# Another order for the end of the second mixer: two pairs of heads in a row, and the convolution's end among the output projection's blocks

## The chip, the cores and the metric

One core of one Trainium2 chip runs the whole program. The metric is the time of one execution in device microseconds: the median of several runs, and beside them one execution that the hardware profiler recorded.

## The reference

The input is 256 rows of 1024 values in float32. The reference sends them through two blocks. The first block has two layers of feed-forward, a mixer of three kinds of attention, and feed-forward. The second block, in which the change lies, has two layers of another mixer (`hybrid_layer`), each of which adds its result to the rows:

```python
o_a = fox_attention(...) * jax.nn.silu(f_gate)             # 4 heads of 64: blocks 0, 1 of the mix
o_b = conformer_conv(glu_in, ...) * jax.nn.silu(c_gate)    # 256 channels: blocks 2, 3
o_c = nsa_attention(...) * jax.nn.silu(n_gate)             # 8 heads of 64: blocks 4 to 7
return x + jnp.concatenate([o_a, o_b, o_c], axis=-1) @ w_out
```

`conformer_conv` gates its input, runs a causal convolution of 31 taps over the 256 rows in each of 256 channels, normalizes each row over its channels, applies SiLU and multiplies by a 256x256 matrix (`conv_pw`). Each head of `nsa_attention` has three terms: compressed keys, the selected keys (at this length all keys) and a window (again all keys). The last two are two causal softmaxes over 256 keys with different keys and values. The mix of 1024 columns is then multiplied by `w_out`, 1024x1024.

## The kernel before

The rows lie in two tiles of 128 partitions. A float32 product is taken as three matmuls of rounded parts: each factor is split into a high part (`L270` or, for weights, `L107`, on ACT) and a low part (`L271`, `L108`, on DVE), and `mm3` (`L237` to `L241`) multiplies low by high, high by high and high by low. Weights come through one stream of blocks (`Stream`): an SP DMA into `raw`, then `L107` and `L108`, with buffers that come round after seven blocks, so that a weight's cast waits for the matmuls of the block seven places earlier. The queues of the engines are filled by a scheduler that takes the order of the program text and a priority for each instruction; what the engine then does is the order that it was given.

A layer of the second mixer runs its input projections first, with some of the 62 taps (31 for each of two halves of the channels, `L1314`, on DVE) put between them: 40 of them are issued by the time that the part begins which the change touches. From there these pieces are in the text:

- `nsa_pair(p)`, two heads: `first` has the scores of the two softmaxes on PE (`L576`, into PSUM tiles `xt` of which there are three), the bias and the running minimum on DVE (`L584`), the exponentials on ACT (`L592`), the reciprocals and the weights on DVE (`L1214`, `L1217`, `L597`). `second` has one matmul for the compressed term (`L1225`, into the one tile `ot`), for each of the four weighted matrices three transposes on PE (`L267`, into an `xt`) and a copy on ACT (`L608`), the products with the values (`L615`, `L617`), and `gated_out` (`L1194`, `L270`, `L271`), which writes block 4 + p of the mix, `mT`, in two parts.
- `attend` issues the `first` of a pair and then the `second` of the pair before it; `settle` issues a `second` that is still waiting.
- `conv(n)` issues the next n taps. `conv_norm` transposes the 256 channels by 256 rows on PE, takes mean and variance of each row (`L1328`, `L1329`, and `L276`, `L277` on POOL) and normalizes into `yn` (`L1331`), one row tile after the other. `conv_silu` transposes back, scales (`L1341`), takes a tanh on ACT (`L1342`), multiplies (`L1344`) and splits into `R` (`L270`, `L271`). `conv_out` has twelve matmuls of 256 columns by `conv_pw` (`L245` to `L247`), then for two blocks `L1356`, `L270` and `L271`, which write blocks 2 and 3 of the mix.
- `outs(j)` multiplies one block of the mix by its 128 rows of `w_out`, in the order `OUT_ORDER = (0, 1, 4, 5, 2, 3, 6, 7)`: twelve matmuls of 512 columns, into four PSUM tiles `acc` that are held for all eight blocks. `finish_phase` has the last four blocks: 24 matmuls for the first row tile, then its residual and norm, then 24 for the second.

Before the change the end of the layer is written as pair 0, all the remaining 22 taps, pair 1, two output blocks, `conv_norm`, pair 2, an output block, `conv_silu`, pair 3, `conv_out`, an output block, the last `second`.

Of the kernel before, what the change touches and what calls it, by code (L numbers as in the profile page):

```python
# [138 lines left out]
class Kernel:  # L139
# [805 lines left out]
    def mixer2_stream(self, l):  # L945
        I, st = self.ins, self.st
        w = I["w_in_2"][l]
        self.xs_spec(w, 2308, 512)
        self.xs_spec(w, 2820, 280)
        self.xs_spec(w, 1796, 512)  # L950

        def with_hidden(c0, n):

            w1 = I[f"cmp_{n}_w1_2"][l].rearrange("(j p) f -> p j f", p=128)
            for i in range(2):
                self.ws_spec(w, c0 + 256 * i, 256)
                for j in (2 * i, 2 * i + 1):
                    st.add(w1[:, 4 * j:4 * j + 4, :], 4, 256)

        with_hidden(1028, "k")  # L960
        self.xs_spec(w, 512, 260)
        with_hidden(0, "v")
        self.ws_spec(w, 3100, 256)
        self.ws_spec(w, 772, 256)
        self.ws_spec(w, 3356, 256)
        self.ws_spec(w, 1540, 256)
        wo = I["w_out_2"][l].rearrange("(k p) f -> p k f", p=128)
        for i, k in enumerate(self.OUT_ORDER):
            if i == 3:
                st.add(I["conv_pw_2"][l].rearrange("(k p) f -> p k f", p=128), 2, 256)  # L970
            st.add(wo[:, k:k + 1, :], 1, 1024)

# [2 lines left out]
    def mixer2(self, l, src, pre, nxt, mid, late):  # L975
# [216 lines left out]
        def gated_out(k, o, gate):  # L1192
            y = self.gt(512)[:, :256]
            nc.vector.scalar_tensor_tensor(y, o, 0.5, gate, op0=OP.mult, op1=OP.mult)  # L1194
            self.split(mT[0][:, k], mT[1][:, k], y)
# [3 lines left out]
        def nsa_pair(p):  # L1199
            g = p // 2  # L1200
            pp = []

            def first():
                pp.extend([self.p384() for _ in range(2)] for _ in range(2))
                s = self.small(24)
                low, den, w = (s[:, i:i + 8].rearrange("p (m i b) -> p m i b", m=2, i=2) for i in (0, 8, 16))
                for i in range(2):
                    sc = self.scores([qT[r, p] for r in HALVES], [kT[r, g, i] for r in HALVES])
                    for m in range(2):
                        self.biased(pp[i][m], sc[m], self.table(4), 1.0, low[:, m, i])  # L1210
                for i in range(2):
                    for m in range(2):
                        self.exps(pp[i][m], low[:, m, i], den[:, m, i])
                nc.vector.reciprocal(s[:, 16:24], s[:, 8:16])  # L1214
                for m in range(2):
                    h = 2 * p + m
                    nc.vector.tensor_tensor(w[:, m], w[:, m],  # L1217
                                            gs[:, :, 3 * h + 1:3 * h + 3].rearrange("p b i -> p i b"), op=OP.mult)
                for i in range(2):
                    for m in range(2):  # L1220
                        self.weighted(pp[i][m], w[:, m, i])

            def second():
                o = self.pair_out()
                nc.tensor.matmul(o(), lhsT=vbd[:, 2 * p:2 * p + 2].rearrange("p a b -> p (a b)"), rhs=pcT,  # L1225
                                 start=True, stop=False)
                pts = [self.turn(pp[i], "aa") for i in range(2)]
                for i in range(2):
                    c = (384, 640)[i] + 64 * g
                    self.values(o, pts[i], [[nk[:, t, c:c + 64] for t in range(2)]] * 2, False, i == 1)  # L1230
                gated_out(4 + p, o(), sn[:, p])

            self.attend((first, second))
# [60 lines left out]
        def silu_gate(dst):  # L1294
            def f(i, a):
                d = dst[:, 2 * i:2 * i + 2]
                t = self.gt(2, 256)
                nc.scalar.activation(t, a, AF.Tanh, scale=0.5)
                nc.vector.scalar_tensor_tensor(d.rearrange("p a b -> p (a b)"), t.rearrange("p a b -> p (a b)"), 1.0,
                                               a.rearrange("p a b -> p (a b)"), op0=OP.add, op1=OP.mult)  # L1300
            return f
# [5 lines left out]
        def conv(n):  # L1307
            for _ in range(min(n, len(taps))):
                f, j = taps.pop(0)
                y = ypad[:, f, j:j + 256]  # L1310
                if j == 0:
                    nc.vector.tensor_scalar(yc[:, f], y, col(f, 0), col(f, 31), op0=OP.mult, op1=OP.add)
                else:
                    nc.vector.scalar_tensor_tensor(yc[:, f], y, col(f, j), yc[:, f], op0=OP.mult, op1=OP.add)  # L1314
# [5 lines left out]
        def conv_norm():  # L1320
            tp = self.cut(self.xt(), (2, 256))
            for t in range(2):
                for f in range(2):
                    self.transpose(tp[:, t, 128 * f:128 * f + 128], yc[:, f, 128 * t:128 * t + 128])
            yn.append(self.sb("yn", [2, 256], 1))
            s = self.small(24)
            for t in range(2):
                nc.vector.bn_stats(s[:, 6 * t:6 * t + 6], tp[:, t])  # L1328
                nc.vector.bn_aggr(s[:, 12 + 2 * t:14 + 2 * t], s[:, 6 * t:6 * t + 6])  # L1329
                self.rstd(s[:, 16 + t:17 + t], s[:, 13 + 2 * t:14 + 2 * t])  # L1330
                nc.vector.tensor_scalar(yn[0][:, t], tp[:, t], s[:, 12 + 2 * t:13 + 2 * t], s[:, 16 + t:17 + t],  # L1331
                                        op0=OP.subtract, op1=OP.mult)
# [28 lines left out]
        def out(i, t):  # L1361
            q = slice(128 * t, 128 * t + 128)
            k = self.OUT_ORDER[i]
            if not d:
                d.extend([self.acc(512), self.acc(512)] for _ in range(2))
            while len(W) <= i:
                W.append(st.next())
            for n in range(2):
                c = slice(512 * n, 512 * n + 512)
                self.mm3(d[t][n], (mT[0][:, k, q], mT[1][:, k, q]), tuple(x[:, 0, c] for x in W[i]), i == 0, i == 7)  # L1370

        def outs(*js):
            for i in js:
                for t in range(2):
                    out(i, t)
# [30 lines left out]
        conv(8)  # L1406
        self.ws_proj3(src, silu_gate(sc_), 0)
        nsa_pair(0)
        conv(62)
        nsa_pair(1)  # L1410
        outs(0, 1)
        conv_norm()
        nsa_pair(2)
        outs(2)
        conv_silu()
        nsa_pair(3)
        conv_out()
        outs(3)
        self.settle()
        self.close_inner()  # L1420
        late()
        self.finish_phase(lambda i, t: out(4 + i, t), 4, d, 1.0, nxt)
# [98 lines left out]
```

## Time and profile before

| | us |
|---|---|
| runs, median of 3 | 1621.61 |
| lowest, highest | 1618.85, 1622.76 |
| profiled execution | 1624.3 |
| span of the profiled execution, first to last instruction | 1622.5 |

The profiled execution lies 2.7 us above the median of the runs, and 1.8 us of it lie around its span. In the span the first block ends at about 1273 us and the first layer of the second block at about 1447 us; its second layer ends with the program. A timeline row gives the start in us from the span's start, the duration, engine, line, operation, output and input with their shapes, how many instructions were merged, and in brackets the idle time of the engine before it and what ended it. The matmuls of PE overlap by pipelining, so a step on PE is best taken from start to start.

### The profile page before, as it was taken

The numbers are of one execution on the slowest core, as the hardware profiler recorded it, in microseconds if no ns is written. First come the engines' busy times: TensorE is split into PE (matmuls) and PEld (weight loads), VectorE is DVE, ScalarE is ACT, GpSimd is POOL, SyncE is SP. The second block draws the span as 40 slices with busy tenths as digits, with TensorE's granted clock in tenths as the row PEclk, the third lists the DMA queues.
The fourth block names the chain that finished last, engine by engine and source line by source line (L and its number), as shares of the span: only waits on it lengthen the run. The fifth ranks groups of instructions, "written<-read, shape, count | busy, mean of one in ns | idle before, by whom it ended". The sixth has DMA issues, their size and how long they took to land.

```text
span 1622.5 us, 23859 instructions
## 1 busy us (share of the span) xinstructions
PE 1576.8 (97%) x8874; PEld 1325.5 (82%) x8874; DVE 1112.3 (69%) x2144; ACT 894.2 (55%) x1619; POOL 45.1 (3%) x66
## 2 busy tenths in 40 slices
PE   7999999999999999999999999999999999899988
PEld 5888888787878888788889787888888799579966
DVE  5756566667776665665656667787566579877985
ACT  5655455566665554555545655765555465555454
POOL 0000000001000000000010001000000000000000
PEclk9999999999999999999999999999999999899989
DMA  8776546454667664766636444468665375137601
GB/s 268 237 230 185 140 134 182 121 143 120 190 212 234 188 192 122 244 191 186 184 98 187 137 134 140 138 207 268 187 194 165 100 209 189 53 83 216 206 29 39
DMA packets 204300, 271.12 MB, mean 167 GB/s; under 512 B 10382, under 2 KB 172056, under 8 KB 204184
## 3 DMA queue, kind: packets, MB, share of 16 engines
q1 hardware_dynamic: 203752, 268.56, 55.9%
q8 instruction: 69, 1.13, 0.3%
q10 hardware_dynamic: 432, 1.05, 0.2%
q14 instruction: 47, 0.39, 0.1%
HBM read 268.52 MB, written 1.05 MB: 166 GB/s over the span
## 4 chain that ended last, share of the span: by engine, by line
PE 82%; DVE 7%; DMA 4%; ACT 4%; issue 2%; POOL 1%; SPq 0%; DVEq 0%; POOLq 0%; ACTq 0%
PE acc L252 28%; PE acc L253 14%; PE xt L241 4%; PE xt L240 4%; PE xt L239 4%; PE xt L267 4%; PE acc L239 3%; PE acc L240 3%; PE acc L241 3%; PE ot L615 2%; PE xt L576 2%; DVE w L108 2%; ACT w L107 2%; PE acc L245 1%; PE acc L247 1%
## 5 line engine op out<-in xcount | busy, mean ns | idle before, releaser
L108 DVE TENSOR_TENSOR w<-raw,w 128x1024 fp32r<-128x1024 f32 (+4 forms) x520 | 610.0, 1180 | 287.2 <-ACT w L107 277.5
L107 ACT CAST w<-raw 128x1024 fp32r<-128x1024 f32 (+4 forms) x520 | 525.5, 1014 | 317.5 <-PE acc L253 92.4
L252 PE MATMUL acc<-h,w 128*128 128x512 f32 x1824 | 649.2, 397 | 0.0
L253 PE MATMUL acc<-h,w 128*128 128x256 f32 x1824 | 515.8, 283 | 0.0
L252 PEld LDWEIGHTS acc<-h,w 128*128 128x128 f32 x1824 | 343.7, 188 | 78.8 <-issue 1.3
L253 PEld LDWEIGHTS acc<-h,w 128*128 128x128 f32 x1824 | 343.0, 188 | 3.8 <-issue 2.5
L239 PE MATMUL acc<-w,h 128*128 128x512 f32 (+5 forms) x448 | 168.4, 377 | 1.5 <-DVE h L271 1.0
L240 PE MATMUL acc<-w,h 128*128 128x512 f32 (+5 forms) x448 | 165.9, 370 | 0.0
L241 PE MATMUL acc<-w,h 128*128 128x512 f32 (+5 forms) x448 | 165.2, 369 | 0.5 <-DVE w L108 0.5
L257 ACT COPY gt<-acc 128x256 f32<-128x256 f32 x240 | 88.3, 373 | 139.1 <-PE acc L253 138.8
L258 DVE TENSOR_TENSOR gt<-gt,acc 128x256 f32<-128x256 f32 x240 | 98.7, 417 | 57.4 <-ACT gt L257 56.4
L239 PE MATMUL xt<-w,R 128*128 128x512 f32 x264 | 103.3, 391 | 1.2 <-DVE R L271 1.2
L240 PE MATMUL xt<-w,R 128*128 128x512 f32 x264 | 103.2, 391 | 0.0
L241 PE MATMUL xt<-w,R 128*128 128x512 f32 x264 | 103.1, 391 | 0.0
L239 PEld LDWEIGHTS acc<-w,h 128*128 128x128 f32 x448 | 85.5, 191 | 20.7 <-DVE h L271 3.8
L241 PEld LDWEIGHTS acc<-w,h 128*128 128x128 f32 x448 | 85.4, 191 | 14.0 <-DVE w L108 1.2
L240 PEld LDWEIGHTS acc<-w,h 128*128 128x128 f32 x448 | 85.3, 191 | 12.4 <-issue 0.5
L592 ACT ACTIVATE p<-p,small 128x128 f32<-128x128 f32 (+1 forms) x176 | 77.9, 445 | 20.5 <-DVE small L584 12.8
L245 PE MATMUL acc<-h,w 128*128 128x256 f32 x256 | 71.8, 281 | 0.0
L246 PE MATMUL acc<-h,w 128*128 128x256 f32 x256 | 71.7, 280 | 0.0
L247 PE MATMUL acc<-h,w 128*128 128x256 f32 x256 | 71.5, 279 | 0.0
L576 PE MATMUL xt<-G 64*128 64x128 f32 (+3 forms) x352 | 55.7, 356 | 5.0 <-DVE small L584 4.4
(256 smaller groups left out, 1926.7 us busy)
## 6 DMA issues: line engine op xcount, KB each, us to landing
raw<-in_w_in_dram SPq DMA_DIRECT2D x144, 512.0 KB, 4.3
raw<-in_ffn_w_gate_dram SPq DMA_DIRECT2D x88, 512.0 KB, 4.5
raw<-in_ffn_w_up_dram SPq DMA_DIRECT2D x88, 512.0 KB, 4.5
raw<-in_ffn_w_down_dram SPq DMA_DIRECT2D x88, 512.0 KB, 4.3
raw<-in_w_out_dram SPq DMA_DIRECT2D x32, 512.0 KB, 3.9
raw<-in_cmp_k_w_dram SPq DMA_DIRECT2D x8, 512.0 KB, 3.7
raw<-in_cmp_v_w_dram SPq DMA_DIRECT2D x8, 512.0 KB, 4.7
raw<-in_w_in_dram SPq DMA_DIRECT2D x8, 416.0 KB, 3.3
```

The costliest lines, as they stand in the source:

```text
L107: nc.scalar.copy(wh, raw)
L108: nc.vector.tensor_sub(wl, raw, wh.bitcast(F32))
L239: nc.tensor.matmul(out, lhsT=al, rhs=bh, start=first, stop=False)
L240: nc.tensor.matmul(out, lhsT=ah, rhs=bh, start=False, stop=False)
L241: nc.tensor.matmul(out, lhsT=ah, rhs=bl, start=False, stop=last)
L245: nc.tensor.matmul(out, lhsT=ah, rhs=bl, start=first, stop=False)
L247: nc.tensor.matmul(out, lhsT=al, rhs=bh, start=False, stop=last)
L252: nc.tensor.matmul(out, lhsT=ah, rhs=rhs, start=first, stop=False)
L253: nc.tensor.matmul(out[:, 1], lhsT=al, rhs=rhs[:, 0], start=False, stop=last)
L257: self.nc.scalar.copy(dst, a[:, 1])
L258: self.nc.vector.tensor_add(dst, dst, a[:, 0])
L576: nc.tensor.matmul(st[m][:, c], lhsT=qs[m][:, at:at + 128], rhs=ks[m][:, 0:n], start=True, stop=True)
```

## The change

The 22 taps that were left are cut in two: ten behind pair 1, the rest behind pair 2. Pair 1 follows pair 0 directly. `conv_norm` comes behind pair 3, an output block is moved ahead of `conv_silu`, and the last `second` ahead of `conv_out`. In the weight stream `conv_pw` trades places with the fourth block of `w_out`, as the new order takes them. The same instructions are issued.

```diff
--- before.py
+++ after.py
@@ -966,7 +966,7 @@
         self.ws_spec(w, 1540, 256)
         wo = I["w_out_2"][l].rearrange("(k p) f -> p k f", p=128)
         for i, k in enumerate(self.OUT_ORDER):
-            if i == 3:
+            if i == 4:
                 st.add(I["conv_pw_2"][l].rearrange("(k p) f -> p k f", p=128), 2, 256)
             st.add(wo[:, k:k + 1, :], 1, 1024)
 
@@ -1406,17 +1406,18 @@
         conv(8)
         self.ws_proj3(src, silu_gate(sc_), 0)
         nsa_pair(0)
+        nsa_pair(1)
+        conv(10)
+        outs(0, 1)
+        nsa_pair(2)
         conv(62)
-        nsa_pair(1)
-        outs(0, 1)
+        outs(2)
+        nsa_pair(3)
         conv_norm()
-        nsa_pair(2)
-        outs(2)
+        outs(3)
         conv_silu()
-        nsa_pair(3)
+        self.settle()
         conv_out()
-        outs(3)
-        self.settle()
         self.close_inner()
         late()
         self.finish_phase(lambda i, t: out(4 + i, t), 4, d, 1.0, nxt)
```

What this makes of the queues is the same in both layers but for single rows; the second layer is shown. First DVE, behind the weights of pair 0 (`L597`). `L1194` and `L271` belong to the heads before that pair; `L584` is the bias of pair 1, and each of its instructions has a second row for the minimum that it reads out; `G` with `conv` as input is a tap. Before:

```order
L597 TENSOR_SCALAR p<-p,small 128x256
L1194 SCALAR_TENSOR_TENSOR gt<-ot,G 128x256
L1314 SCALAR_TENSOR_TENSOR G<-G,conv 128x256 x2
L271 TENSOR_TENSOR h_69<-gt,h_69 128x256
L1314 SCALAR_TENSOR_TENSOR G<-G,conv 128x256 x14
L584 ISA p,small<-xt,base 128x128
L584 ISA small 128x1
L584 ISA p,small<-xt,base 128x256
```

Now:

```order
L597 TENSOR_SCALAR p<-p,small 128x256
L1194 SCALAR_TENSOR_TENSOR gt<-ot,G 128x256
L584 ISA p,small<-xt,base 128x128
L584 ISA small 128x1
L584 ISA p,small<-xt,base 128x256
L584 ISA small 128x1
L271 TENSOR_TENSOR h_69<-gt,h_69 128x256
L584 ISA p,small<-xt,base 128x128
L584 ISA small 128x1
L584 ISA p,small<-xt,base 128x256
```

The sixteen taps that stood ahead of pair 1's bias are gone from there. One of its four biases has moved ahead of the weights of pair 0, and the others follow `L1194`.

Next PE near the layer's end; `p` in `L267` are transposes of a pair's weighted matrices, `G` and `yn` those of the convolution, `w_14174` is the first of the last four blocks of `w_out`. Before, from the last transposes of pair 2 to the first product of `conv_out`:

```order
L267 MATMUL xt<-ident,p 128x128 x3
L615 MATMUL ot<-pt,G 64x256 x2
L617 MATMUL ot<-pt,G 64x128 x2
L615 MATMUL ot<-pt,G 64x256 x2
L617 MATMUL ot<-pt,G 64x128 x2
L245 MATMUL xt<-R,w_14059 128x256
L246 MATMUL xt<-R,w_14059 128x256
L247 MATMUL xt<-R,w_14059 128x256
```

Now, from the end of pair 2's products with the values to the same place:

```order
L617 MATMUL ot<-pt,G 64x128 x2
L267 MATMUL xt<-ident,G 128x128 x4
L1225 MATMUL ot<-G 128x256
L267 MATMUL xt<-ident,yn 128x128
L267 MATMUL xt<-ident,p 128x128 x6
L267 MATMUL xt<-ident,yn 128x128 x3
L267 MATMUL xt<-ident,p 128x128 x6
L615 MATMUL ot<-pt,G 64x256 x2
L617 MATMUL ot<-pt,G 64x128 x2
L615 MATMUL ot<-pt,G 64x256 x2
L617 MATMUL ot<-pt,G 64x128 x2
L245 MATMUL xt<-R,w_14064 128x256
```

The transposes of the convolution (`G` and `yn`) stood among the pairs, far ahead of this place. Now both stand behind the products of pair 2, and the transposes and products of pair 3, which followed `conv_out`, stand among and ahead of it. `conv_out` is followed at once by the last four blocks.

Last ACT, around the tanh of the convolution (`L1342`). Before:

```order
L608 COPY pt<-xt 128x384 x4
L270 CAST h_69<-gt 128x256
L1342 ACTIVATE gt<-gt 128x512
L592 ACTIVATE p,small<-p,small 128x128
L592 ACTIVATE p,small<-p,small 128x256
L592 ACTIVATE p,small<-p,small 128x128
L270 CAST R<-gt 128x512
L592 ACTIVATE p,small<-p,small 128x256
```

Now:

```order
L592 ACTIVATE p,small<-p,small 128x256
L608 COPY pt<-xt 128x384 x4
L270 CAST h_69<-gt 128x256
L608 COPY pt<-xt 128x384 x4
L1342 ACTIVATE gt<-gt 128x512
L270 CAST R<-gt 128x512
L270 CAST h_69<-gt 128x256 x3
```

The tanh stood ahead of pair 3's exponentials. Now it stands behind them and behind eight copies, four of pair 2 and four of pair 3. In the first layer casts of the next weights stand here too: an `L107` ahead of each of two `L270`, and, as before, an `L107` and an `L108` between `L1356` and the `L271` that ends the convolution.

## Rows read from the trace of the kernel before

**Rows 1.** The page, part 1: busy us, share of the span, instructions, by engine.

```profile
PE 1576.8 (97%) x8874; PEld 1325.5 (82%) x8874; DVE 1112.3 (69%) x2144; ACT 894.2 (55%) x1619; POOL 45.1 (3%) x66
```

**Rows 2.** Waits of PE, 1558 to 1623 us: waiter, releaser, us in total, times, longest.

```profile
PE xt L576 <- DVE small L584: 3.0, 1, 3.0
```

**Rows 3.** Windows: length, busy us (records) by engine, granted clock, DMA share, GB/s.

```profile
1394.00:1397.00 3.00, 3.00 (x7) 1.99 (x8) 3.00 (x9) 0.11 (x1) 0.00 (x0) 0.50 0.01 3
...
1573.00:1576.00 3.00, 2.78 (x12) 1.79 (x10) 2.68 (x10) 3.00 (x14) 0.00 (x0) 0.50 0.02 5
...
1576.00:1579.00 3.00, 3.00 (x15) 1.93 (x17) 2.86 (x12) 1.17 (x3) 0.00 (x0) 0.50 0.01 3
...
1606.00:1609.00 3.00, 3.00 (x14) 2.44 (x13) 0.00 (x0) 0.00 (x0) 0.00 (x0) 1.00 0.36 124
```

**Rows 4.** Timeline of DVE, second layer: start, us, engine, line, operation, tiles, count.

```profile
1556.54 0.28 DVE L584 CUSTOM_DVE_ANT_0 p<-xt,base 128x128 f32<-128x128 f32 x1
...
1558.76 1.67 DVE L1314 SCALAR_TENSOR_TENSOR G<-G,conv 128x256 f32<-128x256 f32 x4
...
1562.79 1.92 DVE L597 TENSOR_SCALAR p<-p,small 128x128 f32<-128x128 f32 x8
...
1564.63 0.42 DVE L1194 SCALAR_TENSOR_TENSOR gt<-ot,G 128x256 f32<-128x256 f32 x1
...
1566.08 5.63 DVE L1314 SCALAR_TENSOR_TENSOR G<-G,conv 128x256 f32<-128x256 f32 x14
```

**Rows 5.** Timeline of ACT, second layer.

```profile
1558.14 0.40 ACT L592 ACTIVATE p<-p,small 128x128 f32<-128x128 f32 x1
...
1561.65 0.83 ACT L608 COPY pt<-xt 128x384 f32<-128x384 f32 x2
...
1575.48 1.21 ACT L608 COPY pt<-xt 128x384 f32<-128x384 f32 x3
...
1592.17 0.63 ACT L1342 ACTIVATE gt<-gt 128x512 f32<-128x512 f32 x1 [1.15 <-DVE gt L1341]
...
1596.74 1.59 ACT L608 COPY pt<-xt 128x384 f32<-128x384 f32 x4
```

**Rows 6.** Timeline of DVE, second layer, the convolution's end.

```profile
1580.27 0.43 DVE L1328 BATCH_NORM_STATS2 small<-xt 128x6 f32<-128x256 f32 x1
...
1583.84 0.18 DVE L1329 BATCH_NORM_AGGREGATE small<-small 128x2 f32<-128x6 f32 x1
...
1585.02 0.54 DVE L1331 TENSOR_SCALAR yn<-xt,small 128x256 f32<-128x256 f32 x1 [0.68 <-POOL small L277]
...
1590.74 0.54 DVE L1341 TENSOR_SCALAR gt<-xt,conv 128x256 f32<-128x256 f32 x1 [0.16 <-PE xt L267]
...
1594.61 0.69 DVE L271 TENSOR_TENSOR R<-gt,R 128x512 fp32r<-128x512 f32 x1 [0.18 <-ACT R L270]
...
1600.86 0.76 DVE L1356 SCALAR_TENSOR_TENSOR gt<-xt,G 128x256 f32<-128x256 f32 x2 [0.25 <-PE xt L247]
```

**Rows 7.** Timeline of PE, second layer.

```profile
1564.01 1.66 PE L576 MATMUL xt<-G 64*128 64x128 f32 x8
...
1590.05 0.66 PE L267 MATMUL xt<-ident,yn 128*128 128x128 f32 x4
...
1599.18 0.39 PE L245 MATMUL xt<-R,w 128*128 128x256 f32 x1
...
1604.49 0.50 PE L240 MATMUL acc<-w,h 128*128 128x512 f32 x1
```

**Rows 8.** Timeline of PE, first layer, the first of the last 48 matmuls.

```profile
1434.77 0.50 PE L239 MATMUL acc<-w,h 128*128 128x512 f32 x1
```

**Rows 9.** Timeline of ACT, first layer.

```profile
1426.62 1.58 ACT L608 COPY pt<-xt 128x384 f32<-128x384 f32 x4
...
1430.74 1.05 ACT L107 CAST w<-raw 128x1024 fp32r<-128x1024 f32 x1 [0.71 <-PE xt L247]
```

**Rows 10.** Timeline of DVE, first layer.

```profile
1431.82 1.22 DVE L108 TENSOR_TENSOR w<-raw,w 128x1024 fp32r<-128x1024 f32 x1
```

## The prediction

> **What bounds the kernel now.** I read the page first: PE is busy for 97% of the span [rows 1], so time can only come from PE's waits and from its clock. The waits of PE at the second layer's end come next: its longest is 3.0 us, on the bias `L584` [rows 2]. The DVE timeline shows why: pair 1's scores run on PE from 1564.01 and take 1.66 us [rows 7], but DVE has fourteen taps from 1566.08 to 1571.7 ahead of the bias [rows 4]. The table by windows gives the second half of the cost: after the wait the granted clock is 0.50, the lower of the two levels (1.2 of 2.4 GHz), from 1573 to 1579, with PE busy nearly all the while [rows 3]. Last I read each engine's queue around the places that change, because all engines work their queues in order here.
>
> My reference in each layer is the moment when 48 matmuls of the output projection are left, all of `finish_phase`: from there on both kernels do the same. In the first layer that is 1434.77 [rows 8]. In the second 47 are left at 1604.49 [rows 7]; one matmul is 0.23 us at the full clock (13 weight loads in 3 us [rows 3]), so the moment is 1604.26.
>
> **What the change removes: taps ahead of pairs.** I add up DVE's new queue with durations of the second layer. A tap is 0.40 (5.63 by 14), the bias of a pair 2.22 (1556.54 to 1558.76), the weights of a pair 1.84 (1562.79 to 1564.63), `L1194` with `L271` 0.65 (1564.63 to 1566.08 less two taps) [rows 4], a weight's `L108` 1.2 [rows 10]. Reciprocal and `L1217` are 0.34: from the copies' start at 1561.65 [rows 5], which follows the last exponential, to 1562.79, less two taps. The exponentials of a pair take 3.5 on ACT (1558.14 to 1561.65) [rows 5]. The first of pair 1's four biases now falls into DVE's wait for pair 0's exponentials, so nothing moves until pair 0's weights end at 1564.63. Then:
>
> - `L1194`, `L271` and three biases; the last of these needs the third and fourth score tile, half as much again on PE as before (1564.01 + 2.5 = 1566.5), so DVE has done them by about 1567.6 and four taps by 1569.2.
> - Pair 1's last exponentials stand on ACT behind pair 0's first copy and end at about 1569.6. Reciprocal, tap, `L108`, weights: 1573.4.
> - `L1194`, `L271`, pair 2's bias: 1576.3. Its exponentials begin at about 1574.4 and end at 1577.9; 0.34, three taps, weights: about 1581.0.
> - `L1194`, `L271`, nine taps: 1585.3. Then pair 3's bias; its exponentials start 0.6 later and end at **1589.4**.
>
> Before they end at 1596.74, where the copies begin [rows 5]. So pair 3's softmax comes 7.3 us earlier. In the first layer two casts of 1.05 us [rows 9] stand ahead of `L270` on ACT and the clock is at its lower level for longer (0.50 at 1394 to 1397 [rows 3]); I take 1.5 us for that and get 1419.5 against 1426.62 [rows 9].
>
> **What it adds: a serial end.** Before, from pair 3's exponentials to the reference it is 7.5 us (1596.74 to 1604.26) and 8.15 us (1426.62 to 1434.77): copies, values, `conv_out`, and pair 3's transposes and values, behind which `conv_out`'s last steps are hidden. The norm of the convolution had been finished long before. Now the convolution's transposes stand on PE behind pair 2's values, and pair 2's copies on ACT behind pair 3's exponentials. From 1589.4 on each step waits for the one before it:
>
> 1. Copies, pair 2's values, transposes, until `L1328`: 4.8 us where the same steps ran mostly at the lower clock (1575.48 [rows 5] to 1580.27 [rows 6]); at the full clock 2.44 (1596.74 to 1599.18 [rows 5, 7]) and 0.7 for the transposes, 3.2.
> 2. The norm of two row tiles, DVE and POOL: 5.3 before (1580.27 to 1585.56), of which pair 2's biases between made up about 0.9; 4.4. From `L1329` to `L1331` it is 1.18 each time [rows 6].
> 3. Three transposes of `p`, whose PSUM tile is the one the norm has just read, then the last three of `yn`, until `L1341`: four transposes with the handover are 0.69 (1590.05 [rows 7] to 1590.74 [rows 6]) at the full clock; so 1.1, or 1.7 at half.
> 4. `L1341` twice: 1.0 [rows 6]. PSUM tiles are short again: pair 3's last six transposes need the tile that `L1341` reads, and the tanh stands on ACT behind their copies: 0.15 + 0.69 + two copies of 0.40 (1.21 by 3 [rows 5]), 1.5 to 2.1.
> 5. Tanh to the end of the split: 1592.17 [rows 5] to 1595.30 [rows 6], 3.1 with exponentials between; 2.9 to 3.1.
> 6. `conv_out` to the first matmul of the next block: 1.68 to `L1356` (1599.18 to 1600.86 [rows 7, 6]) and 1.4 for `L1356`, `L270`, `L271` and the handovers, 3.1; at half clock 4.4.
>
> The trace of before has no 256-column matmul at the lower clock; I bound step 6 by the full rate and by twice it. The Trainium skill ("TensorE: Matmul & The Clock Gate", section "Wait — 56ns, not 53.3ns?") gives columns over 1.2 GHz from start to start at that level, 0.213 us for 256 columns; by it the twelve take an estimated 2.6 us where the row has 1.4, and the step 4.3.
>
> The sum is 17.2 at the full clock and 21.5 at the lower one. PE mostly waits in this stretch, and after a wait of 3.0 us the row shows the lower clock; but it starts from the full one. I take **19.3**, near the middle. The first layer has a cast and an `L108` more in steps 1 and 6 (1.05 and 1.2 [rows 9, 10], half of it beside other work): 2.3 more, 21.6.
>
> Second layer: 1589.4 + 19.3 = 1608.7, against 1604.26: 4.4 later. First layer: 1419.5 + 21.6 = 1441.1, against 1434.77: 6.3 later.
>
> **The last 48 matmuls.** Before they run at 1.00 throughout. Now they start behind a wait on `L271`, at a clock that has seen little work. A half-clock stretch lasted at least 6 us [rows 3], and in it 7 matmuls run where else 13 do, so it takes half of its time. I take 4.5 us of it, 2.2 lost in each layer; bounds are 0 and 3.0.
>
> Moving the weights costs nothing: `conv_pw` and one block of `w_out` trade places on SP's queue, and the waits in these stretches are for PE, ACT and DVE, not for a transfer; if it were late, ACT's cast would hold up the copies behind it by as much. POOL's queue keeps its order.
>
> Sum: 4.4 + 6.3 + 2 x 2.2 = 15.1. On the profiled 1624.3 us that is 1639.4; that execution is 2.7 above the median, so **1636.7 us**.
>
> **Rivals.**
> - *The clock stays up.* If PE's waits are too short to lower it, the end costs 17.2 and 19.5: 1606.6 and 1439.0, 2.3 and 4.2 later, and the last 48 lose nothing: 1630.8 profiled, 1628 in the median. For it: the wait that lowers the clock before is one of 3.0 us, and the new ones are of 1 to 3. Against: there are five in a row.
> - *Gain and loss cancel.* The end breaks even at 14.9 us in the second layer and 15.3 in the first, some 2 to 4 below my full-clock sums. It needs pair 3's softmax to be done 2 us earlier than my DVE sum, which holds only 1 to 2 us of idle time, or the norm to be shorter. Then about 1622.
> - *The gain is kept: faster.* If the convolution's norm, tanh and split were done beside pair 3's softmax, the end would be 7.5 and 8.15 us as before, and all 7.3 and 7.1 us stay: 1607. It is decided by when `L1328` starts: at the last tap, 1585.3, or behind pair 2's values, 1592 to 1594. For it: the taps do end before pair 3's exponentials. Against it: the row of transposes on PE.
>
> **Chances.** Forecast 0.57, clock stays up 0.21, cancel 0.15, kept 0.07. What a measurement of this kernel can tell from no change is about 0.3%, 4.9 us. The first two cases lie above it but for a small part of the second: slower 0.76, same 0.16, faster 0.08. The forecast's own range, from a clock that is up most of the time to the lower one throughout (ends of 21.5 and 23.8: 6.6 and 8.5 later, and twice 3.0: 21.1 more), is 1629 to 1643. For 8 in 10 I go down into the cancelling case, to 1624, and up to 1644.
>
> **What would show it.** Right: the 3.0 us wait on `L584` is gone, pair 3's exponentials end 6 to 8 us earlier, near 1589 and 1419; behind them PE waits for copies, for `L1331` at the `yn` transposes, for the split before `L245`, and for `L271` at the first of the last blocks, with a granted clock of 0.50 in parts of it. Step by step: 19 us from pair 3's exponentials to the last 48 matmuls where it was 7.5. Wrong: exponentials that end after 1592 (the sum on DVE is too low) or before 1587; an end of under 15 us (the serial chain is not serial); the last 48 at 1.00 (no clock lost). In the median, a time under 1622 would refute the chain.

## The result and the profile after

The changed kernel takes 1633.03 us, median of 4 runs (1630.72 to 1634.08), against 1622.18 of the kernel before beside it: a ratio of 1.0072, 95% interval 1.0060 to 1.0085, or 10.9 us slower. In a second set it was 1631.57 (6 runs), ratio 1.0059 (1.0044 to 1.0074). The forecast was 1636.7 with a range of 1624 to 1644. The profiled execution took 1633.98 us, 1632.2 of it span. The work on PE is the same to a tenth [rows 1]:

```profile
PE 1576.8 (97%) x8874; PEld 1327.1 (81%) x8874; DVE 1111.8 (68%) x2144; ACT 894.0 (55%) x1619; POOL 51.0 (3%) x66
```

PE's busy time holds what the lower clock costs in either kernel, so the 9.7 us by which the span is longer are time in which PE waits. These are PE's waits after the change, waiter, releaser, us in total, times, longest; first the longest three of the first layer (1385 to 1455 us), then all of the second (1563 to 1633):

```profile
PE xt L267 <- DVE yn L1331: 3.2, 2, 3.0
PE acc L239 <- DVE h L271: 2.7, 1, 2.7
PE ot L615 <- ACT pt L608: 2.3, 1, 2.3
...
PE ot L615 <- ACT pt L608: 2.3, 1, 2.3
PE xt L267 <- DVE yn L1331: 1.9, 1, 1.9
PE xt L245 <- DVE R L271: 1.9, 1, 1.9
PE acc L239 <- DVE h L271: 1.4, 1, 1.4
PE xt L267 <- ACT pt L608: 1.1, 2, 0.6
```

The 3.0 us on `L584` [rows 2] are gone. In their place stand waits on the steps of the convolution: on `L1331` ahead of the `yn` transposes, on `R` ahead of `conv_out` and on the last `L271` ahead of the last 48 matmuls. (The 2.3 us on `L608` stand there before the change too.)

One new wait lies outside the part that the edit touches. In the first layer PE waits for a small copy on POOL (`L1149`, of the compressed keys), which took 1.94 us before the change:

```profile
1331.37 7.73 POOL L1149 COPY G<-G 32x64 f32<-32x64 f32 x1 [54.17 <-DVE G L1017]
```

```profile
PE xt L267 <- POOL G L1149: 2.7, 1, 2.7
```

A second profile of the changed kernel has 7.74 us and a wait of 2.4. From the copy's start to pair 0's copies on ACT it is 58.2 us in both, where it was 57.0. Whether the edit is what lengthens this copy is open; the last section comes back to it.

ACT after the change, the copies behind pair 3's exponentials in the first layer, and the same and the tanh in the second [rows 5, 9]:

```profile
1421.41 1.63 ACT L608 COPY pt<-xt 128x384 f32<-128x384 f32 x4
...
1597.57 1.63 ACT L608 COPY pt<-xt 128x384 f32<-128x384 f32 x4
...
1608.00 0.63 ACT L1342 ACTIVATE gt<-gt 128x512 f32<-128x512 f32 x1
```

DVE in the second layer, the steps of the serial end [rows 6]:

```profile
1600.73 0.43 DVE L1328 BATCH_NORM_STATS2 small<-xt 128x6 f32<-128x256 f32 x1 [0.16 <-PE xt L267]
...
1604.75 0.54 DVE L1331 TENSOR_SCALAR yn<-xt,small 128x256 f32<-128x256 f32 x1 [1.00 <-POOL small L277]
...
1606.29 1.00 DVE L1341 TENSOR_SCALAR gt<-xt,conv 128x256 f32<-128x256 f32 x2 [0.99 <-PE xt L267]
...
1610.04 0.69 DVE L271 TENSOR_TENSOR R<-gt,R 128x512 fp32r<-128x512 f32 x1 [0.35 <-ACT R L270]
```

PE: in the first layer the first of the last 48 matmuls and where they speed up, in the second the first and last product of `conv_out` and the first of the last 48 [rows 7, 8]:

```profile
1440.11 0.74 PE L239 MATMUL acc<-w,h 128*128 128x512 f32 x1 [2.73 <-DVE h L271]
...
1443.21 0.58 PE L240 MATMUL acc<-w,h 128*128 128x512 f32 x1
1443.63 0.39 PE L241 MATMUL acc<-w,h 128*128 128x512 f32 x1
...
1610.88 0.36 PE L245 MATMUL xt<-R,w 128*128 128x256 f32 x1 [1.86 <-DVE R L271]
...
1612.25 0.28 PE L247 MATMUL xt<-R,w 128*128 128x256 f32 x1
1613.94 0.50 PE L239 MATMUL acc<-w,h 128*128 128x512 f32 x1 [1.41 <-DVE h L271]
```

Windows of PE there: length, busy us (records), granted clock, DMA share, GB/s [rows 3].

```profile
1439.00:1442.00 3.00, 1.89 (x5) 0.70 0.55 131
1442.00:1445.00 3.00, 3.00 (x11) 0.73 0.02 8
1603.00:1606.00 3.00, 2.12 (x10) 0.67 0.00 0
1606.00:1609.00 3.00, 3.00 (x24) 0.76 0.00 0
1614.00:1617.00 3.00, 3.00 (x13) 1.00 0.00 0
```

Read so: from pair 3's last exponential to the last 48 matmuls it is 18.7 us in the first layer (1421.41 to 1440.11) and 16.4 in the second (1597.57 to 1613.94), where it was 8.15 and 7.5. In the first layer the last 48 start at the lower clock level, 0.42 us from one to the next until 1443.63; the residual behind the first 24 of them starts 6.74 us after the first, where it was 5.20, so 1.54 us are lost. In the second layer they run at 1.00 and lose nothing.

### The profile page after: what moved, and what is told of

Its sections match the earlier page's. It is cut to its first block, busy times and chain, and to the rows that moved or that the text cites. A ratio compares the mean times of both kernels' runs of the same rounds, so it can differ in the third digit from the quotient of the medians.

```text
span 1632.2 us, 23863 instructions
## 1 busy us (share of the span) xinstructions
PE 1576.8 (97%) x8874; PEld 1327.1 (81%) x8874; DVE 1111.8 (68%) x2144; ACT 894.0 (55%) x1619; POOL 51.0 (3%) x66
## 5 line engine op out<-in xcount | busy, mean ns | idle before, releaser
L108 DVE TENSOR_TENSOR w<-raw,w 128x1024 fp32r<-128x1024 f32 (+4 forms) x520 | 609.9, 1179 | 285.2 <-ACT w L107 276.6
L107 ACT CAST w<-raw 128x1024 fp32r<-128x1024 f32 (+4 forms) x520 | 525.3, 1014 | 318.9 <-PE acc L253 91.3
L239 PEld LDWEIGHTS xt<-w,R 128*128 128x128 f32 x264 | 49.6, 188 | 13.6 <-DVE R L271 3.0
```

Source lines behind the costliest of these rows:

```text
L107: nc.scalar.copy(wh, raw)
L108: nc.vector.tensor_sub(wl, raw, wh.bitcast(F32))
L239: nc.tensor.matmul(out, lhsT=al, rhs=bh, start=first, stop=False)
```

## The experiments

All differences below are against the kernel before, run on the same chip in the same set; its median was 1620.0 to 1621.4. In brackets stand the ratio and its 95% interval; the letters are those of the theories in the expectations. The yardstick inside a trace is the *stretch*: from pair 0's last exponentials to pair 3's, taken between their reciprocals (`L1214`).

**The end alone.** Taps and pairs as before, the end as after:

```diff
         nsa_pair(0)
         conv(62)
         nsa_pair(1)
         outs(0, 1)
-        conv_norm()
         nsa_pair(2)
         outs(2)
-        conv_silu()
         nsa_pair(3)
-        conv_out()
+        conv_norm()
         outs(3)
+        conv_silu()
         self.settle()
+        conv_out()
```

> Late end alone: the taps and pairs stand as before the change (all 22 taps behind pair 0), only the convolution's norm, tanh, output and the last second stand behind pair 3 as after it. Theory A (a serial end that gives back an early gain): pair 3's exponentials end where they did before the change (1596.7 and 1426.6 in its trace), and the whole end of 16.4 and 18.7 us measured after the change stands in place of 7.5 and 8.15, so 8.9 and 10.5 us more, and 0 to 3 us of lower clock in the last 48 matmuls: about 21 us above the kernel before, 1643 (1639 to 1647). Rival B (the early taps and pairs brought nothing, the end alone makes the whole difference): 10.9 us above it, 1633 (1630 to 1636).

Measured: 1635.88, +14.6 us (ratio 1.0090, 1.0076 to 1.0103), between A and B. A's end was there: 19.8 and 15.6 us. What A had wrong is the stretch, which should have kept its length. Second layer, the reciprocals of pairs 0 and 3; before:

```profile
1561.78 0.20 DVE L1214 RECIPROCAL small<-small 128x8 f32<-128x8 f32 x1 [1.35 <-ACT p L592]
...
1596.87 0.20 DVE L1214 RECIPROCAL small<-small 128x8 f32<-128x8 f32 x1 [1.02 <-ACT p L592]
```

with the end alone late:

```profile
1569.20 0.20 DVE L1214 RECIPROCAL small<-small 128x8 f32<-128x8 f32 x1 [1.35 <-ACT p L592]
...
1599.24 0.20 DVE L1214 RECIPROCAL small<-small 128x8 f32<-128x8 f32 x1 [1.67 <-ACT p L592]
```

35.1 us became 30.0 (and 36.3 became 30.0 in the first layer), with the sixteen taps still ahead of pair 1. The early softmax came with the late norm, not with the taps. The last 48 lost 1.8 and 2.3 us to the clock. (The whole change costs 4 us less than its end alone; the 2.3 us of the second layer, which the changed kernel doesn't lose, are the part of that seen in the traces.)

**The early pairs alone.** Pairs and taps as after, the norm and the tanh ahead of pair 3, the rest of the end as before:

```diff
         nsa_pair(2)
         conv(62)
+        conv_norm()
         outs(2)
+        conv_silu()
         nsa_pair(3)
-        conv_norm()
-        outs(3)
-        conv_silu()
-        self.settle()
         conv_out()
+        outs(3)
+        self.settle()
```

> Early pairs alone: pair 1 straight behind pair 0 and the taps cut in two as after the change, but the convolution's norm behind its last tap and ahead of pair 3, its tanh ahead of pair 3, its output and the last second as before the change. Theory A: the end is 7.5 and 8.2 us again; the norm's 4.4 us now stand ahead of pair 3's bias, of which about 1 us lies beside the wait for scores, so pair 3's exponentials end 3.3 and 1 us earlier than before the change: 4 us below the kernel before, 1618 (1613 to 1621). Rival B (the 6.8 and 4.5 us by which the exponentials came earlier never reach the output projection): 1622 or more. Rival C (the norm lies wholly beside pair 3's softmax): all 11 us are kept, 1611.

Measured: 1628.76, +7.5 us (1.0044, 1.0030 to 1.0058). A's forecast fails: with the norm back in it the stretch is 37.3 and 35.5 us, nothing earlier at all. In the second layer the granted clock falls as well, and the end takes 10.1 us where it was 7.5; three rows of windows (us, busy of PE, PEld, DVE, ACT and POOL, clock, DMA share, GB/s):

```profile
1590.00:1595.00 5.00, 3.03 (x10) 1.83 (x12) 2.52 (x10) 0.88 (x4) 1.58 (x4) 0.70 0.01 2
1595.00:1600.00 5.00, 4.82 (x21) 3.25 (x21) 3.80 (x16) 3.99 (x17) 0.00 (x0) 0.50 0.01 3
1600.00:1605.00 5.00, 4.57 (x23) 3.15 (x24) 2.75 (x12) 2.01 (x6) 0.00 (x0) 0.50 0.00 0
```

B's 1622 or more holds, C's 1611 does not. The two profiles lie 5.7 us apart. From pair 0's copies to the last 48 matmuls the two layers account for 0.9 and 3.0 us of it, and pair 0 comes 0.9 earlier in the first layer. The other 2.8 lie between the layers, which the edit doesn't touch: there PE waits 1.9 us for `L1124` where it was 1.2, and behind that wait the granted clock is 0.62 and 0.81 (1523 to 1526 and to 1529) where it was 1.00. Why that wait is longer here is open.

**The taps alone.** The kernel before with one line moved:

```diff
         nsa_pair(0)
-        conv(62)
         nsa_pair(1)
+        conv(62)
         outs(0, 1)
```

> The kernel before with one line moved: pair 1 ahead of the remaining taps, which now follow it in one piece; the convolution's norm, tanh and output, the stream and the output blocks stand as before. Theory D, formed on the runs so far (from pair 0's exponentials to pair 3's the length of the stretch is DVE's whole work in it, 29.5 us of 35.1, so that the place of the taps counts little, and the earlier softmax of the changed kernel came from the norm, the tanh's inputs and the split having left the stretch): the same work, so pair 3's exponentials end within 2 us of where they did, and the time is 1621 (1618 to 1624). The prediction's step (taps ahead of pair 1 hold up the pairs by 7.3 and 7.1 us): 14 us less, 1607. Rival F (with the taps later the norm's waits on POOL fall between pairs 1 and 2 with nothing beside them): 3 to 5 us more, 1625.

Measured: 1624.40, +4.4 us (1.0025, 1.0015 to 1.0034): 0.4 above D's range, 17 us from the prediction's step. Second layer, the same two reciprocals:

```profile
1562.22 0.20 DVE L1214 RECIPROCAL small<-small 128x8 f32<-128x8 f32 x1 [1.19 <-ACT p L592]
...
1599.14 0.20 DVE L1214 RECIPROCAL small<-small 128x8 f32<-128x8 f32 x1 [1.02 <-ACT p L592]
```

36.9 us, and 37.6 in the first layer: 1.8 and 1.3 longer than before. With the wait on `L584` shortened (2.0 us in two, longest 1.3) pair 3 comes later, not earlier. D had the stretch right, to the 2 us that it allowed. F's 3 to 5 us fit the time but not the place: DVE waits for POOL ahead of `L1331` twice 0.68 us before and 0.69 and 0.68 here. What is longer here are DVE's waits behind pair 1, 1.66 us for its exponentials (`L1214`) and 1.51 for ACT ahead of an `L271`.

**The changed kernel again.**

> The changed kernel once more, unaltered, with more runs and a second profile, to see how far one profile stands for the kernel. Theory D (what brought pair 3's softmax forward is the norm's place; the 1.8 us by which the place of the taps seemed to move it are the scatter of one execution): from pair 0's last exponentials to pair 3's 28 to 32 us in both layers, not 31.9 and 28.2 again; 16 to 19 us from there to the last 48 matmuls, 0 to 2.6 us of lower clock in them; time 1632 (1629 to 1635). Rival K (the lengths belong to the order of the queues): 31.9 and 28.2 again within 0.3, 18.7 and 16.4 behind them, 1633.

Measured: 1631.57, +10.2 us. The stretch is 30.6 and 31.0 us where the first profile had 31.9 and 28.2; the end 19.4 and 17.0; the last 48 lose 1.5 and 0 again. So 1 to 3 us of the length of a stretch are the scatter of single executions (the two second layers ran at a granted clock of 0.94 and 0.84 in it): D, and K falls. Over all kernels with the norm behind pair 3's bias and the 22 taps in the stretch (nine traces, two layers each; in four second layers the reciprocal stands behind a part of the norm, which adds 0.8 to 1.8 us) it is 28.2 to 32.7 us wherever the taps stand, and with the norm ahead of pair 3 (three traces) 35.1 to 37.6.

**The norm earlier in the serial end.** The changed kernel, with `conv_norm` called at the end of pair 3's `first`, ahead of pair 2's `second`:

```diff
-        def nsa_pair(p):
+        def nsa_pair(p, then=lambda: None):
...
                     self.weighted(pp[i][m], w[:, m, i])
+                then()
...
-        nsa_pair(3)
-        conv_norm()
+        nsa_pair(3, conv_norm)
```

> The changed kernel with one step earlier: the transposes and the norm of the convolution stand between pair 3's scores and pair 2's transposes, so that the norm need not wait for pair 2's values and for ACT. Theory A: the norm of the first row tile runs beside pair 3's exponentials, that of the second ends behind pair 3's weights; from pair 3's exponentials to the last 48 matmuls it is about 12 us where it was 16.4, and about 14 where it was 18.7: 9 us less than the changed kernel with 0 to 1.6 us of clock, 1623 (1619 to 1627). Rival B (what costs is the convolution's output and the lower clock behind it, not the norm's place): 0 to 2 us less, 1631 to 1633.

Measured: 1626.75, +5.5 us (1.0036, 1.0022 to 1.0051), about 5 us less than the changed kernel, where A had 9 and B 0 to 2: the end is 16.7 and 13.1 us, A's direction with a little over half its size. What it missed is the first layer, where the waits that are left come in a row; PE's waits from 1400 to 1455 us:

```profile
PE acc L239 <- DVE h L271: 2.7, 1, 2.7
PE xt L245 <- DVE R L271: 2.6, 1, 2.6
```

Behind them the last 48 start at 0.50, and lose 2.6 us where it was 1.5.

**Other blocks in the waits.**

```diff
-    OUT_ORDER = (0, 1, 4, 5, 2, 3, 6, 7)
+    OUT_ORDER = (0, 1, 4, 5, 6, 7, 2, 3)
```

> The changed kernel with the output projection's blocks in another order: those of pairs 2 and 3 ahead of the convolution's two. Twelve matmuls of pair 2's block can then stand in the waits of the serial end, and twelve of pair 3's block hide the last step from the convolution's output to the mix. Theory A (PE waits in the end while DVE, ACT and POOL work): 2.8 us of matmuls go into waits in each layer, and the waits on the last split (1.4 and 2.7 us) go: 9.7 us less than the changed kernel, 1623 (1619 to 1627); the norm's start stays where it is. Rival B (PE itself is the bound of the end, and each filler delays the chain by its own length): only the waits on the last split go, 4.1 us less, 1629. Rival D (row tile 0's residual and norm are then covered by six matmuls fewer, and the start of the next phase waits for them): 2 to 3 us of it is lost again, 1625 to 1626.

Measured: 1622.74, +1.5 us (1.0012, 1.0001 to 1.0022): A, to 0.3 us in the sum. Twelve matmuls of pair 2's block now run inside the end, and the waits on `yn`, `R` and the last split shrink; PE from 1575 to 1625 us, where the changed kernel had 1.9, 1.9 and 1.4:

```profile
PE xt L267 <- DVE yn L1331: 0.9, 2, 0.5
...
PE xt L245 <- DVE R L271: 0.3, 1, 0.3
PE acc L239 <- DVE h L271: 0.2, 1, 0.2
```

The norm starts no earlier behind pair 3's copies than in the changed kernel (3.2 us); the chain is as long, but PE has work beside it. D's wait is there as well: in the first layer the next phase starts behind 2.3 us on `L271`, where the kernel before has no such wait.

```profile
1448.85 0.50 PE L239 MATMUL acc<-w,h 128*128 128x512 f32 x1 [2.33 <-DVE h L271]
```

This one edit takes back nearly the whole loss all the same.

**Both of these edits, and the taps where they were.**

> Both single edits together on the changed kernel: the convolution's transposes and norm between pair 3's scores and pair 2's transposes, and the output blocks of pairs 2 and 3 ahead of the convolution's two. Theory A (waits of a serial end, to be shortened or filled): against the kernel with the earlier norm alone (1626.8) the two waits on the last split go (2.7 and 1.4 us), six matmuls of pair 2's block fill 1.1 to 1.4 us of the wait for the split in each layer, and the 2.6 us of lower clock in the first layer's last 48 matmuls with them: 1618 (1615 to 1622). Rival I (the two edits fill the same waits, so the second brings nothing beside the first): 1622 to 1624, as the other order of blocks alone.

Measured: 1618.92, 1.1 us below the kernel before (0.9984, 0.9973 to 0.9995). A. The same with all 22 taps behind pair 0, as before the change:

> The kernel of the two edits together (norm between pair 3's scores and pair 2's transposes, blocks of pairs 2 and 3 ahead of the convolution's), but with the taps and pairs where they stood before the change: all 22 taps behind pair 0, ahead of pair 1. Theory D (the place of the taps counts little, 1.8 us either way from pair 0's to pair 3's exponentials, since DVE's work in that stretch is the same): within 2 us of the same kernel with the taps cut, and up to 2 us more for the wait of about 2 us on pair 1's bias and the lower clock behind it: 1620 (1617 to 1623), where that kernel took 1618.9. The prediction's step (taps ahead of the pairs cost 7 us in each layer): 14 us more, 1633.

Measured: 1620.37, -0.1 us (0.9995, 0.9986 to 1.0003): D, in its number; the step's 14 us are not there. The traces are less even than that: the stretch is 31.9 and 32.7 us here and 29.0 and 30.0 in the kernel of both edits. So with all taps ahead of pair 1 it is 2.7 to 2.8 us longer, where the taps alone, moved the other way, had made it 1.3 and 1.8 longer; both are as large as the scatter of one execution.

**The two row tiles of the norm side by side.**

```diff
             for t in range(2):
                 nc.vector.bn_stats(...); nc.vector.bn_aggr(...); self.rstd(...)
+            for t in range(2):
                 nc.vector.tensor_scalar(yn[0][:, t], ...)
```

On the changed kernel:

> The changed kernel with one step of its end shortened: the two row tiles of the convolution's norm are taken side by side (both statistics first, then both normalizations), so that the second's statistics run on DVE while POOL works on the first. Theory A (every step of the end stands on the path that sets the end): from the first L1328 to the end of the second normalization 3.3 us where it was 4.56 and 4.37, 1.2 us less in each layer and 2.4 in all, 1630.6 (1629 to 1632). Rival J (the norm is hidden in part beside pair 3's transposes and copies, and something else comes last): 0 to 1 us, 1632 to 1633.

Measured: 1627.88, +7.4 us (1.0053, 1.0035 to 1.0070), 3.5 and 2.8 us less than the two sets of the changed kernel by the medians and 3 and 1 by the ratios, with intervals that overlap. DVE in its second layer:

```profile
1594.30 0.76 DVE L1328 BATCH_NORM_STATS2 small<-xt 128x6 f32<-128x256 f32 x2 [0.16 <-PE xt L267]
...
1596.83 1.06 DVE L1332 TENSOR_SCALAR yn<-xt,small 128x256 f32<-128x256 f32 x2 [1.29 <-POOL small L277]
...
1599.22 0.99 DVE L1342 TENSOR_SCALAR gt<-xt,conv 128x256 f32<-128x256 f32 x2 [1.33 <-PE xt L267]
...
1603.20 0.42 DVE L1194 SCALAR_TENSOR_TENSOR gt<-ot,G 128x256 f32<-128x256 f32 x1 [0.92 <-PE ot L617]
```

The norm is 1.0 us shorter (1594.30 to 1597.89), but from pair 3's copies to `conv_out` only 0.2 of it arrives (13.15 us against 13.31): DVE's `L1194` of pair 3 stands ahead of the split into `R` and now waits 0.92 us for pair 3's products. That is J in the trace; the size in the medians is open. On the kernel of both edits:

> The kernel of the two edits together with the two row tiles of the norm side by side. In it the second normalization stood behind pair 3's weights; now both stand ahead of them, which puts the weights 0.5 us later and the tanh about 1 us earlier. Theory A: the tanh and the split set the start of the convolution's output, so 0.5 to 1.5 us less in each layer, 1617 (1615 to 1619). Rival J (pair 3's weights and transposes come last there): 0 to 1 us more, 1619.5.

Measured: 1618.30, 2.2 us below the kernel before (0.9985, 0.9976 to 0.9994): no more than both edits alone within the intervals. A's range holds it, but so would no gain at all. It and the kernel of both edits are the only two whose intervals lie wholly below the kernel before, by 1 to 2 us.

**Fewer taps in the stretch.** Twelve of the 22 taps among the input projections, on the kernel before and on that of both edits:

```diff
+        conv(12)
         self.xs_proj(src, 260, fox_v)
```

> The kernel before with twelve taps more issued earlier, among the input projections (between the second gated input and the projection of the values of the first attention), where DVE is idle for 7 us of 20; ten are left behind pair 0. Theory D: 12 taps of 0.41 us, 4.9 us of DVE's work, leave the stretch from pair 0's to pair 3's exponentials, whose PE work of 31.1 us allows at most 4 us; 3 us gained in each layer, 1615 (1612 to 1619). Rival G (the taps stand ahead of the low parts of the weights there, and PE waits in the projections for as much): 1621 or more. Rival H (PE, not DVE, is the bound of the stretch): 0 to 2 us, 1620.

> The kernel of the two edits together (norm between pair 3's scores and pair 2's transposes, blocks of pairs 2 and 3 ahead of the convolution's), and twelve taps issued earlier, among the input projections. Theory D: the stretch to pair 3's exponentials is 3 to 4 us shorter again in each layer, and the norm then lies earlier beside it: 7 us below the kernel without the earlier taps, 1611 (1606 to 1616). Rivals G and H as for the earlier taps alone: 1618 or more.

Measured: 1634.51, +14.5 us (1.0084, 1.0071 to 1.0097), and 1640.39, +20.4 (1.0118, 1.0105 to 1.0131). Inside the stretch D holds, with more than its size: 30.2 and 29.5 us where it was 36.3 and 35.1, for 4.6 us less work on DVE in each; with both edits 25.3 and 27.9 where it was 29.0 and 30.0. H, which had PE as the bound and at most 2 us to gain, falls. But far from there PE now waits 6.8 and 6.9 us for `L1149`, the copy on POOL. POOL, with the taps early:

```profile
1511.26 9.88 POOL L1149 COPY G<-G 32x64 f32<-32x64 f32 x1 [55.47 <-ACT w L107]
```

and in the kernel before:

```profile
1503.99 0.38 POOL L1149 COPY G<-G 32x64 f32<-32x64 f32 x1 [53.13 <-ACT G L1251]
```

Behind each wait PE runs at the lower level for some 5 to 6 us; in the first layer (length, PE busy, clock, DMA share, GB/s):

```profile
1342.00:1348.00 6.00, 5.40 (x25) 0.50 0.83 260
```

In the traces pair 0's copies come 10.9 us later than before in the first layer, and the way from there to the second layer's adds 11.6: 22.5 us lost ahead of pair 0, of which the two waits are 13.7 and the lower clock behind them is a further part. From pair 0's copies to the last 48 matmuls 11.4 us are won back, and the two profiles lie 11.1 apart. So G is right that it is lost in the projections, and wrong on what waits. Fewer taps in the stretch at a place clear of that copy were not tried.

## Why the prediction was right, and which of its steps were not

The mechanism and the sign hold: an earlier softmax, a serial end that takes back more, 10 to 11 us in all. From pair 0's copies to the last 48 matmuls the two profiles of the changed kernel have 50.2 and 46.3 us on average, before it was 44.5 and 42.6: 5.7 and 3.7 later, and 1.5 of clock, 10.9 together. (The wait for `L1149` lies ahead of pair 0 and is not in this sum.) The steps:

- *What the change removes: taps ahead of pairs.* The size was near: stretches of 27.75 and 29.2 us were forecast in the second and first layer, and 29.6 and 31.2 came, about 2 us too little in each. The name was wrong, and this is the step that failed. The sum over DVE's new queue left the taps in and the norm, `L1341`, `L1344` and the split out, and I put the whole difference down to the taps. Moved alone, the taps lengthen the stretch; with the end alone moved it is 5.0 and 6.3 us shorter. Before, second layer (window, its length, busy us of PE, PEld, DVE, ACT and POOL, clock, DMA share, GB/s):

```profile
1561.65:1596.74 35.09, 31.08 (x164) 20.67 (x165) 29.48 (x117) 18.38 (x67) 1.58 (x4) 0.85 0.00 1
```

  with the end alone late:

```profile
1569.07:1599.12 30.05, 25.88 (x151) 18.39 (x152) 25.21 (x107) 16.99 (x65) 0.00 (x0) 0.90 0.00 1
```

  and with twelve taps early:

```profile
1578.20:1607.86 29.66, 29.10 (x168) 19.58 (x168) 24.83 (x106) 17.93 (x65) 1.58 (x4) 0.90 0.00 1
```

  DVE is busy for 84% in the first two. What leaves its queue with the late end (4.3 us of work here, and the waits for POOL ahead of `L1331`) shortens the stretch by about as much. That run alone doesn't part DVE from PE, which is busy for more of the stretch than DVE (a part of it at the lower clock) and loses 13 of its 164 matmuls with the norm. The twelve early taps do: PE has four matmuls more there, DVE 4.6 us less, and the stretch is 5.4 us shorter by these windows. PE is then busy for 29.10 of 29.66 us, so DVE no longer holds it up there. What only changes places in the stretch moved it by 1 to 3 us, longer in both trials. The wait of 3.0 us on `L584` that led me to the taps was where PE showed DVE's load, not what caused it.
- *Steps 1 to 6 of the end.* Second layer 3.16, 4.56, 1.00, 1.71, 2.88 and 3.06 us, 16.4; first layer 4.40, 4.37, 0.99, 1.71, 2.88 and 4.35, 18.7. Against the full-clock sum of 17.2, step 4 is the one that was too long: pair 3's transposes and copies run beside `L1341`, and 2.5 was their sum. The first layer's cast and `L108` cost 1.2 and 1.3 us in steps 1 and 6, near the 2.3 taken for both.
- *The clock in them, 19.3 where 17.2 was the full-clock sum.* Mis-sized by all of it. Most of the end is spent on DVE, ACT and POOL, and there PE's clock costs nothing; the second layer's rows show 0.67 and 0.76 only from 1603 to 1609 (in the first layer it is 0.50 from 1430 to 1433), and `conv_out` ran at the upper level, eleven steps from 1610.88 to 1612.25, 0.125 us each. The Trainium skill ("TensorE: Matmul & The Clock Gate", section "Wait — 56ns, not 53.3ns?") gives the columns over 1.2 GHz from start to start, by which 256 columns take an estimated 0.213 us at the lower level. The run with the end alone late agrees: in its first layer the eleven steps of `conv_out` were one of 0.35 us and ten of 0.213 to 0.214, at a granted clock of 0.50 (window, length, PE busy, clock, DMA share, GB/s). So twice the rate was the right upper bound of step 6; the changed kernel did not come to it. That the trace of before has no 256-column matmul at the lower clock was misread: pair 2's products (`L615`) stand there at 0.50, two in 0.43 us from 1577.31.

```profile
1432.64:1435.13 2.49, 2.49 (x11) 0.50 0.02 7
```

- *The last 48 matmuls, 2.2 us in each layer.* 1.5 in the first, 0 in the second, in both profiles; 1.8 and 2.3 with the end alone late, 2.6 and 0 with the earlier norm. Within the bounds of 0 and 3.0, and not a number that one layer foretells for another.
- *Rivals.* The clock stays up (1628) had the end right for the second layer. It was outweighed by a stretch that came 2 us less early than forecast. In each layer the two errors, an end too long by 2.6 us and a gain too large by 2, mostly cancelled, and that is luck: over both layers the ends were 5.2 us too long, the gains 3.9 too large and the last 48 2.9 too dear, which leaves the 4.2 between 15.1 and 10.9. The gain kept (1607) needs the norm beside the softmax; the run with the norm just behind pair 3's bias, the nearest to it, came to 1626.8.
- *The cancelling case* (about 1622) needed ends of 15.3 and 14.9 us; they were 18.7 and 16.4.
- *What would show it.* The wait on `L584` is gone and the waits named are there. In the trace's own time pair 3's exponentials end at 1597.57, past the 1592 that was to show a wrong sum; but the layer's pair 0 comes 7.7 us later, and counted from there it is 1589.9. Over both profiles the softmax came 5.5 and 5.1 us earlier, less than the 6 to 8 named. That the second layer's last 48 lost no clock was named as a sign against, and came.
- *Moving the weights costs nothing; POOL's queue keeps its order.* No wait in either layer's end is for a transfer. The order on POOL stayed; a copy in it became longer in the first layer, which the sum did not have.

## What to carry to other kernels

When a wait on an engine's queue is followed back to what stands ahead in the queue, ask what the engine's whole work between two fixed points is: here only work that left the stretch shortened it, and reordering within it did not. Look at the other engines in the same windows too, and ask whether work for them leaves with it. In this serial end of small steps on several engines, independent work for the engine that waits helped more than a shorter step: the order of the output blocks took back about 9 us, and a norm shorter by 1.0 us hardly 0.2 of it. Compare a stretch over several traces before a difference of 2 us in one is believed.

## What the runs showed of the hardware that was not expected

The copy of 32x64 on POOL, `L1149`, took 9.73 and 9.88 us (both layers) with the twelve early taps, and 7.73 and 0.37 in the changed kernel, where it took 1.94 and 0.38 before. Each time it was long, it ended when DVE, which had run instructions without a gap, first stood idle. DVE in the kernel with the early taps: the instruction that was running when the copy began, the last of the series and the next:

```profile
1511.20 1.21 DVE L108 TENSOR_TENSOR w<-raw,w 128x1024 fp32r<-128x1024 f32 x1
...
1520.96 0.20 DVE L1260 SCALAR_TENSOR_TENSOR G<-G 128x8 f32<-128x8 f32 x1
1521.54 0.18 DVE L1156 COPY G<-xt 64x32 f32<-64x32 f32 x1 [0.38 <-PE xt L267]
```

The copy ran from 1511.26 to 1521.14. In the first layer of the changed kernel it ran from 1331.37 to 1339.11, and DVE's series ended at 1339.12; before the change a gap of 0.07 us on DVE, behind four taps, let it end at 1335.21. In the second layer of both kernels DVE goes on without a gap for 8 us, but its next instruction has one input, and the copy is over in 0.37 and 0.38 us. The Trainium skill ("SBUF — State Buffer", section "Who interferes with whom") states that a DVE instruction with two inputs in SBUF contends with a GpSimd instruction that reads SBUF. The trace agrees, and shows more: the copy stayed blocked over a whole series of such instructions, short ones with one input among them. That DVE's series is the cause is read from these coincidences and was not tested by itself. DVE's queue around the copy is the same before and after the change. Of the twelve traces without the early taps six have the short copy in the first layer (1.94 or 1.95 us) and six a long one (6.53 to 7.74), so whether the edit or the single execution decides it is open.
